# A hybrid decoder layer: value transposes six products earlier, and the down stage's first operands queued behind the last channel tile

## The chip, the cores and the metric

The kernel runs on one core of a Trainium2 chip. The metric is the device time of one execution in microseconds (us); less is better. The core's engines work side by side and wait for one another through semaphores: TensorE (PE in the profile, with its weight loads as PEld), VectorE (DVE), ScalarE (ACT), GpSimd (POOL) and SyncE (SP), which here issues all DMAs.

## What is computed

One decoder layer on 1040 tokens (16 learned meta tokens and 1024 of input), width 1024, all in float32. Two groups of four heads run side by side on one input projection: differential attention (two softmax maps, subtracted) and HGRN2 (a gated linear recurrence). Their outputs are joined, projected and added to the residual; a feed-forward layer with a short convolution follows. Cut to what matters:

```
a = rmsnorm(h, ln_mix_pre)
dq, dk, dv, hq, hf, hi, hg = jnp.split(a @ w_in, SPLITS, axis=-1)
mix = concat([diff_attention(dq, dk, dv, ...), hgrn2(hq, hf, hi, hg, ...)]) @ w_out
h = h + rmsnorm(mix, ln_mix_post)
u = rmsnorm(h, ln_ffn_pre) @ w_up                  # 1024 -> 2 x 2816
u = causal_conv_width_3(u) + conv_b                # per channel
gate, up = jnp.split(u, 2, axis=-1)
y = (gelu(gate) * up) @ w_down                     # 2816 -> 1024
return (h + rmsnorm(y, ln_ffn_post))[meta tokens dropped]
```

## The kernel before

Every float32 operand of a large product is split into a high part (a cast on ACT) and the rest (a subtraction on DVE or POOL), and each product is three matmuls: high by high, high by rest, rest by high. PE's order is the order in which the code issues its instructions (`manual_schedule`). The order of the other engines, SP's included, is planned when the program is built: among the instructions that are ready by the planner's own times, the one issued first in the code goes first, unless an edge holds it. `issue_after(x)` draws such an edge: what the block issues on the engine of `x` is queued behind `x`, without a wait for its end. `high_priority` moves a block ahead of what is issued before it. On the chip each engine then keeps its planned order. A tile gets a buffer of its tag in the same planning; its first writer waits until the tile that had the buffer is read out.

*The heads.* For each head a dense part (`dense`, L726) and a side part (attention or HGRN2) are interleaved on PE: each step of the side part is followed by dense products of about so much cost. The dense part computes transposed projections, tile by tile of 128 channels; a tile has three groups of tokens (`proj_group`, L191), a group 24 products (eight slices of the width by three matmuls, L203, L205 and L207) into a PSUM bank `pi_...`. For the value tiles, `dv` of the attention and `hi` of HGRN2, the result is copied to SBUF by ACT (`vt`, `ht`) and noted in a list `late`; `flush` (L369) later transposes it in blocks of 128 tokens on PE (`to_nat`, L311, products L317 and L319) into a bank `pn_va` or `pn_vh`, from which ACT copies it to its place (`avn`, `vn`). The flush of a group stands behind the 15th product of the group that comes next (`step == 14`, L734). The bank of the transposes is of the tag "m", which in this stage has two; the same tag serves the attention's late scores `E` (L639), its transposed probabilities `pt` (L666), its output `pa` (L690), the transposes of the normed outputs `ss` and `ssa` (L518), and HGRN2's `pk`, `pu` and `pl`. There are 24 flushes: two of head 0's `dv` stand in another function (`head0`, L900), four in the first group of a dense part, 18 elsewhere in `dense`.

*The up projection* works on 22 tiles of 128 channels of each half (`ft`, loop L1384), in two halves of the tokens `p`. From tile 1 on a tile is seven block products by a Strassen-like scheme (`unit`, L1305, steps j = 0 to 6, in `mm` L1311 twelve matmuls each) in the banks `pa`, `pb`, `pc`, which DVE and ACT combine between the steps (`u2` L1326, `u3` L1332, the copy of `ug` L1336). `prep` (L1077) casts and sums the weights of the next tile. At the end of a tile `gated` (L1279) convolves on ACT and DVE, multiplies on POOL and stores the result to DRAM (`gsc`, L1284). Beside tiles 6 to 20 `down_sums` (L1371) prepares sums of the down weights with buffers of the tag "gk".

*The down stage* has seven products by the same scheme (`ORDER`, L1400), each over 11 channel tiles: 77 steps, of 12 matmuls (L1483 to L1485). A step's operands (`operands`, L1433) are a tile of `gsc` (`g_in`, tag "gk", four buffers), a tile of weights (`w_in`, tag "ra", five buffers, which the up projection's raw weights use before), their casts `gh` and `wh` on ACT and the rests `gl` and `wl` on DVE; `gh` and `gl` have four buffers, `wh` shares four with the up projection. The code issues the operands of a step three steps ahead of its products (`ahead`, `LOOK`, L1548), those of the first three after the up projection's loop, the first with high priority. Between them `sums5` (L1427) loads three more tiles per channel tile. No edge holds these loads and casts, so that they go as early as the planner has buffers for them.

## Time and profile before

| | |
|---|---|
| median of 3 runs | 1334.59 us (1334.57 to 1335.59) |
| the profiled execution | 1334.41 us |
| its span, first to last instruction | 1332.6 us |
| its mean granted TensorE clock | 0.995 |
| head stage, with the joined output projection begun | about 60 to 560 us of the span |
| up projection | about 660 to 1106 us |
| down stage | 1106 us to the end |

Times in the views are counted from the start of the span. A group or row names line, engine, operation, the tile written and the tiles read; DVE, ACT and POOL instructions are recorded under the line of the helper that issues them (L54), so they are told apart by their tiles. A timeline row has start and duration in us, and in brackets the engine's idle time ahead of it with what ended it. Matmuls overlap in the pipeline, so their durations are longer than their distance.

### The profile page before, as it was taken

To read this page: it belongs to the slowest core of one execution; us is meant where nothing else is said; L and a number is where in the kernel's file an instruction comes from. 1 tells how busy PE (TensorE), PEld (TensorE's weight loads), DVE (VectorE), ACT (ScalarE), POOL (GpSimd) and SP (SyncE) were. 2 spreads that over 40 slices of the span, in tenths; PEclk is the share of its full clock that TensorE was granted. 3 is DMA by queue.
4 is the path that set the end of the run, shared out by engine and by line. 5 is a ranking of instruction groups with operands and counts; after the bars stand their busy time and mean duration, and the time that the engine had idled before them with its cause. 6 is when DMAs were issued, how large, how long until landed. Compare 5 with 4: busy or idle time off the path is not lost.

```text
span 1332.6 us, 26191 instructions
## 1 busy us (share of the span) xinstructions
PE 1288.0 (97%) x10172; PEld 1187.6 (89%) x10172; DVE 931.6 (70%) x1531; ACT 692.5 (52%) x1635; POOL 456.2 (34%) x340
## 2 busy tenths in 40 slices
PE   8999999999999999899999999999999989999997
PEld 7899999899999988677999999999999988878875
DVE  6464646465645664547997788988989886697586
ACT  8465466447544755246754444444444444454553
POOL 5211211121112110344076667677676630010121
PEclk9999999999999999999999999999999999999999
DMA  6111111112111234587232224545445436955363
GB/s 208 61 41 32 54 56 41 48 45 64 44 41 33 88 100 152 170 265 265 83 111 80 80 96 152 181 147 163 162 147 170 156 120 214 329 176 166 88 205 119
DMA packets 99427, 165.00 MB, mean 124 GB/s; under 512 B 10035, under 2 KB 34899, under 8 KB 99302
## 3 DMA queue, kind: packets, MB, share of 16 engines
q1 hardware_dynamic: 99302, 163.32, 37.8%
q8 instruction: 80, 1.31, 0.4%
q14 instruction: 45, 0.37, 0.1%
HBM read 122.65 MB, written 40.63 MB: 123 GB/s over the span
## 4 chain that ended last, share of the span: by engine, by line
PE 43%; DVE 10%; DMA 4%; issue 3%; ACT 3%; POOL 1%; SPq 0%; DVEq 0%; ACTq 0%; POOLq 0%
PE pd L1484 5%; PE pd L1483 5%; PE pd L1485 5%; PE pb L1316 4%; DVE c L54 3%; PE pb L1317 3%; PE pb L1318 3%; PE pa L1316 2%; PE pa L1317 2%; PE pa L1318 2%; PE pc L1316 2%; PE pc L1317 2%; PE pc L1318 2%; DMA gi<-gsc 1%; DVE ul L54 1%
## 5 line engine op out<-in xcount | busy, mean ns | idle before, releaser
L1316 PE MATMUL pb<-t,uh 128*128 128x258 f32 x504 | 144.8, 287 | 11.9 <-DVE u L54 11.8
L1317 PE MATMUL pb<-t,uh 128*128 128x258 f32 x504 | 142.3, 282 | 0.0
L1318 PE MATMUL pb<-t,ul 128*128 128x258 f32 x504 | 142.3, 282 | 0.0
L1484 PE MATMUL pd<-wl,gh 128*128 128x512 f32 x308 | 122.0, 396 | 0.5 <-DVE wl L54 0.5
L1483 PE MATMUL pd<-wh,gh 128*128 128x512 f32 x308 | 121.7, 395 | 0.0
L1485 PE MATMUL pd<-wh,gl 128*128 128x512 f32 x308 | 121.7, 395 | 0.0
L54 POOL TENSOR_TENSOR c<-c,c 128x514 f32<-128x514 f32 (+1 forms) x44 | 74.9, 1702 | 120.6 <-ACT c L54 110.3
L1316 PEld LDWEIGHTS pb<-t,uh 128*128 128x128 f32 x504 | 96.1, 191 | 15.2 <-DVE u L54 15.0
L54 DVE SCALAR_TENSOR_TENSOR c<-uu,cwt,c 128x514 f32<-128x514 f32 (+1 forms) x88 | 87.6, 1004 | 22.6 <-ACT c L54 22.3
L1317 PEld LDWEIGHTS pb<-t,uh 128*128 128x128 f32 x504 | 96.3, 191 | 0.0
L1318 PEld LDWEIGHTS pb<-t,ul 128*128 128x128 f32 x504 | 95.9, 190 | 0.0
L1316 PE MATMUL pa<-t,uh 128*128 128x258 f32 (+1 forms) x336 | 95.2, 283 | 0.0
L1318 PE MATMUL pa<-t,ul 128*128 128x258 f32 (+1 forms) x336 | 95.0, 283 | 0.0
L1317 PE MATMUL pa<-t,uh 128*128 128x258 f32 (+1 forms) x336 | 94.8, 282 | 0.0
L1316 PE MATMUL pc<-t,uh 128*128 128x258 f32 (+1 forms) x336 | 94.4, 281 | 0.0
L1317 PE MATMUL pc<-t,uh 128*128 128x258 f32 (+1 forms) x336 | 94.0, 280 | 0.0
L1318 PE MATMUL pc<-t,ul 128*128 128x258 f32 (+1 forms) x336 | 93.7, 279 | 0.0
L54 DVE SCALAR_TENSOR_TENSOR c<-ug,cwt,c 128x514 f32<-128x514 f32 (+1 forms) x88 | 88.2, 1002 | 1.5 <-ACT c L54 1.4
L54 ACT CAST uh<-ra 128x512 fp32r<-128x512 f32 x67 | 41.0, 616 | 67.9 <-PE pb L1317 49.7
L54 POOL TENSOR_TENSOR ul<-ws,uh 128x512 fp32r<-128x512 f32 x42 | 63.8, 1519 | 27.1 <-ACT uh L54 27.1
L1484 PEld LDWEIGHTS pd<-wl,gh 128*128 128x128 f32 x308 | 57.7, 187 | 15.8 <-DVE wl L54 1.9
L1483 PEld LDWEIGHTS pd<-wh,gh 128*128 128x128 f32 x308 | 57.7, 187 | 14.1
(373 smaller groups left out, 4169.5 us busy)
## 6 DMA issues: line engine op xcount, KB each, us to landing
ra<-in_wup_dram SPq DMA_DIRECT2D x88, 256.0 KB, 3.0
mp<-msc SPq DMA_DIRECT2D x23, 512.0 KB, 5.5
wd<-in_wdown_dram SPq DMA_DIRECT2D x44, 256.0 KB, 3.3
tsc<-wd SPq DMA_DIRECT2D x44, 256.0 KB, 3.1
wi<-tsc SPq DMA_DIRECT2D x44, 256.0 KB, 2.8
gi<-gsc SPq DMA_DIRECT2D x33, 256.0 KB, 3.6
wi<-in_wdown_dram SPq DMA_DIRECT2D x33, 256.0 KB, 4.2
gsc<-c SPq DMA_DIRECT2D x22, 257.0 KB, 2.3
```

The costliest lines, as they stand in the source:

```text
L54: ins = call(*args, **kw)
L1316: T.matmul(pt, hi[:, s], th[:, k], start=(first and k == 0), stop=False, skip_group_check=True)
L1317: T.matmul(pt, hi[:, s], tl[:, k], start=False, stop=False, skip_group_check=True)
L1318: T.matmul(pt, lo[:, s], th[:, k], start=False, stop=(k == 3), skip_group_check=True)
L1483: T.matmul(py, gh[:, s], wh, start=(k == 0 and pr not in (3, 7)), stop=False, skip_group_check=True)
L1484: T.matmul(py, gh[:, s], wl, start=False, stop=False, skip_group_check=True)
L1485: T.matmul(py, gl[:, s], wh, start=False, stop=(k == NH - 1), skip_group_check=True)
```

## The change

Two things. In `dense`, the flush stands behind the 9th product of a group, but for the first group of a dense part, where it stays behind the 15th.

For the down stage, the loads of the first three steps are issued at j = 1 of the last channel tile, on SP behind the store of the tile before it; their casts at j = 4, 5 and 6 of the last tile, on ACT behind the copy of `ug` of that tile's second half. The subtractions on DVE have no edge. The high priority of the first step goes. `ahead` no longer runs for the first three steps. The functions of the down stage are moved ahead of the loop for that, unchanged but for an argument of `operands` by which it takes loaded tiles.

```
             for g in range(3):
                 for step, c in enumerate(proj_group(g, parts, name, evac)):
-                    if step == 14:
+                    if step == (8 if idx or g else 14):
                         flush()
                     yield c
...
-        SY.dma_start(gsc[P * ft: P * (ft + 1), C0[p]:C0[p] + 2 * WN[p] - 2], cg)
+        marks["store"] = SY.dma_start(gsc[P * ft: P * (ft + 1), C0[p]:C0[p] + 2 * WN[p] - 2], cg)
...
-        A.copy(ug[:, :n], pa)
+        marks["left"] = A.copy(ug[:, :n], pa)
...
+    def operands(pr, k, loaded=None):
...
         if pr == 1:
-            a = g_in(k, 0, "1")
+            a = loaded[0] if loaded else g_in(k, 0, "1")
...
-        b = w_in(pr, k)
+        b = loaded[1] if loaded else w_in(pr, k)
...
             if (ft, j) == (1, 1):
                 with tc.issue_after(marks[1, 1].ins):
                     next(p1)
+            if ft == NF - 1 and j == 1:
+                with tc.issue_after(marks["store"].ins):
+                    opens = [(g_in(k, 0, "1"), w_in(1, k)) for k in range(LOOK)]
+            if ft == NF - 1 and j > 3:
+                with tc.issue_after(marks["left"].ins):
+                    ready[j - 4] = operands(1, j - 4, opens[j - 4])
...
     def ahead(i):
         if i < len(steps):
-            with tc.high_priority() if i == 0 else nullcontext():
-                ready[i] = operands(*steps[i])
+            ready[i] = operands(*steps[i])
...
-    LOOK = 3
-    for i in range(LOOK):
-        ahead(i)
     for i, (pr, k) in enumerate(steps):
         ahead(i + LOOK)
```

More of the change, by code (lines that the diff above doesn't have):

```diff
@@ L1381, in down_sums @@
                 yield
-    wd_sums = down_sums()
-    for ft in range(1, NF):
-        units = [unit(ft, p, ps_b) for p in range(2)]
-        for j in range(7):
-            prep(7 * (ft + 1) + j)
-            for u in units:
-                next(u)
-            if ft >= SUMS and j in (1, 3, 5, 6):
-                with tc.issue_after(marks["last"].ins):
-                    next(wd_sums, None)
-            if (ft, j) == (1, 1):
-                with tc.issue_after(marks[1, 1].ins):
-                    next(p1)
-    close(t2_cm, t_cm, xu_cm, mx_cm)
-    f_cm, fp = pool("fin", 1)
-    NH, TAIL = NF // 2, 3
-    ORDER = (1, 2, 5, 6, 3, 7, 4)
-    keep = {nm: fp.tile([P, NH, 512], F32, tag=nm, name=nm) for nm in ("ga", "gb", "gc", "gs")}
-    c11 = fp.tile([P, 4, 512], F32, tag="c11", name="c11")
-    x5 = fp.tile([P, 4, 512], F32, tag="x5", name="x5")
-    gfo = fp.tile([P, D], F32, tag="gfo", name="gfo")
-    ssd = fp.tile([P, 8, 2], F32, tag="ssd", name="ssd")
-    x1 = ep.tile([P, 4, 512], F32, tag="e0", name="x1")
-    u2 = ep.tile([P, 4, 512], F32, tag="e1", name="u2")
-    SY.dma_start(gfo, gfpost.to_broadcast([P, D]))
+    NH = NF // 2
+    LOOK = 3
+    ORDER = (1, 2, 5, 6, 3, 7, 4)
+    keep, ready = {}, {}
     def g_src(k, half):
@@ L1425, in w_in @@
         return t
-    def sums5(k):
-        SY.dma_start(keep["gc"][:, k], g_src(k, 1))
-        b = g_in(k + NH, 1, "5")
-        V.tensor_tensor(keep["gs"][:, k], keep["gc"][:, k], b, op=ALU.add)
-        SY.dma_start(keep["ga"][:, k], g_src(k, 0))
-    def operands(pr, k):
-        ga, gb, gc, gs = (keep[nm][:, k] for nm in ("ga", "gb", "gc", "gs"))
+    def operands(pr, k, loaded=None):
+        ga, gb, gc, gs = (keep[nm][:, k] if keep else None for nm in ("ga", "gb", "gc", "gs"))
         if pr == 1:
-            a = g_in(k, 0, "1")
+            a = loaded[0] if loaded else g_in(k, 0, "1")
         elif pr == 2:
@@ L1461, in operands, with sums5 @@
         return gh, gl, wh, wl
+    wd_sums = down_sums()
+    for ft in range(1, NF):
+        units = [unit(ft, p, ps_b) for p in range(2)]
+        for j in range(7):
+            prep(7 * (ft + 1) + j)
+            for u in units:
+                next(u)
+            if ft >= SUMS and j in (1, 3, 5, 6):
+                with tc.issue_after(marks["last"].ins):
+                    next(wd_sums, None)
+            if (ft, j) == (1, 1):
+                with tc.issue_after(marks[1, 1].ins):
+                    next(p1)
+            if ft == NF - 1 and j == 1:
[4 more added lines that the diff above has]
+                    ready[j - 4] = operands(1, j - 4, opens[j - 4])
+    close(t2_cm, t_cm, xu_cm, mx_cm)
+    f_cm, fp = pool("fin", 1)
+    TAIL = 3
+    keep.update({nm: fp.tile([P, NH, 512], F32, tag=nm, name=nm) for nm in ("ga", "gb", "gc", "gs")})
+    c11 = fp.tile([P, 4, 512], F32, tag="c11", name="c11")
+    x5 = fp.tile([P, 4, 512], F32, tag="x5", name="x5")
+    gfo = fp.tile([P, D], F32, tag="gfo", name="gfo")
+    ssd = fp.tile([P, 8, 2], F32, tag="ssd", name="ssd")
+    x1 = ep.tile([P, 4, 512], F32, tag="e0", name="x1")
+    u2 = ep.tile([P, 4, 512], F32, tag="e1", name="u2")
+    SY.dma_start(gfo, gfpost.to_broadcast([P, D]))
+    def sums5(k):
+        SY.dma_start(keep["gc"][:, k], g_src(k, 1))
+        b = g_in(k + NH, 1, "5")
+        V.tensor_tensor(keep["gs"][:, k], keep["gc"][:, k], b, op=ALU.add)
+        SY.dma_start(keep["ga"][:, k], g_src(k, 0))
     steps = [(pr, k) for pr in ORDER for k in range(NH)]
@@ L1466, in layer_kernel @@
         early.setdefault(min(3 + 3 * k, 2 * NH - 3 + k), []).append(k)
-    ready = {}
     def ahead(i):
         if i < len(steps):
-            with tc.high_priority() if i == 0 else nullcontext():
-                ready[i] = operands(*steps[i])
+            ready[i] = operands(*steps[i])
         for k in early.get(i, []):
```

## The prediction

> **What bounds the kernel now.** I read the page's head first, then the busy time by stage, then TensorE's (PE's) timeline for its idle places.

> ```profile
> span 1332.6 us, 26191 instructions
> PE 1288.0 (97%) x10172; PEld 1187.6 (89%) x10172; DVE 931.6 (70%) x1531; ACT 692.5 (52%) x1635; POOL 456.2 (34%) x340
> ```
> ```profile
> 60.00:440.00 380.00, 370.99 (x3713) 356.78 (x3712) 214.34 (x475) 210.76 (x615) 66.80 (x69) 1.00 0.16 47
> 1120.00:1150.00 30.00, 30.00 (x131) 24.07 (x130) 19.23 (x30) 15.28 (x27) 0.00 (x0) 1.00 1.02 366
> ```

> A row of the second view gives the stage, its length, then the busy time of PE, PEld, DVE, ACT and POOL, the granted clock, the DMA share and GB/s. PE is the bound: in the whole span it stands still for 44.6 us (1332.6 - 1288.0), for 9.0 (380.00 - 370.99) in most of the heads, for nothing in the first down steps although the DMA is full there. So the change can win only places where PE waits. Those that it touches:

> ```profile
> 105.21 0.55 PE L670 MATMUL pt<-ident,pb 128*128 128x128 f32 x3 [0.31 <-ACT vn L54]
> 116.16 0.66 PE L670 MATMUL pt<-ident,pb 128*128 128x128 f32 x4 [0.49 <-ACT pb L54]
> 174.15 0.33 PE L317 MATMUL pn_va<-ident,vt 128*128 128x128 f32 x1 [0.62 <-ACT kn L54]
> 238.65 0.55 PE L319 MATMUL pn_vh<-ident,ht 128*128 128x128 f32 x3 [1.67 <-ACT pb L54]
> 428.30 0.33 PE L317 MATMUL pn_va<-ident,vt 128*128 128x128 f32 x1 [0.62 <-ACT kn L54]
> 494.19 0.90 PE L319 MATMUL pn_vh<-ident,ht 128*128 128x128 f32 x3 [2.53 <-ACT pb L54]
> 1072.97 0.39 PE L1316 MATMUL pb<-t,uh 128*128 128x258 f32 x1 [3.47 <-DVE u L54]
> ```

> The bracket is PE's idle time before the row and who ended it. The value transposes (`pn`) wait not for their source (`ht`, `vt`) but for a PSUM bank: the tag "m" has two, and the transposes got the one from which ACT still had to read scores (`pb` is the exponent) or `kn`. The wait of 0.62 is there three times (first and last shown, heads 1 to 3), the one at 238.65 in head 2 as well.

> ```profile
> 493.70:497.20 3.50, 3.01 (x12) 3.02 (x13) 0.32 (x2) 1.44 (x6) 0.00 (x0) 0.51 0.33 81
> 1074.00:1077.40 3.40, 3.40 (x17) 3.28 (x16) 3.40 (x4) 0.00 (x0) 3.31 (x3) 0.50 0.59 188
> ```

> The two longest waits are each paid twice: around both the granted clock is half for some 3.4 us.

> **First edit: transposes after the 9th product instead of the 15th.** It moves 18 of the 24 flushes (12 of `hi`, 6 of `dv`) up by six products; nothing is added. Each is three transposes. What counts is which banks are busy at the new place.

> *Free places.* In the second `dv` group the 9th product lies four microseconds ahead of the 15th, in front of the products that fill both banks; the banks have been read out there, so the 0.62 goes: 3 x 0.62 = 1.9 us. At 105.21 another tile waits for the copy of the transposed block; that copy comes earlier, 0.3 us. The third `hi` flush of each head (in the first `hg` group), the first one of heads 1 to 3 and the second `dv` ones wait nowhere now, and a bank is free at their new place too: 0.

> *Heads 1 to 3, second `hi` flush.* Head 1:

> ```profile
> 234.03 0.34 PE L207 MATMUL pi_hi<-ahi,wl_hi 128*128 128x384 f32 x1
> 234.05 0.58 ACT L54 ACTIVATE ona<-ssa,sub 128x384 f32<-128x384 f32 x1 [1.03 <-PE ssa L537]
> 234.90 0.38 PE L694 MATMUL pa<-avn,az 128*128 128x128 f32 x2
> 235.08 0.62 ACT L54 CAST wh_dq<-wr_dq 128x512 fp32r<-128x512 f32 x1
> 235.87 1.23 DVE L54 TENSOR_TENSOR ast<-ast 128x1 f32<-128x1 f32 x1
> 238.40 0.20 ACT L54 ACTIVATION_READ_ACCUMULATOR pb<-E,ast 128x1 f32 x1
> 239.24 0.48 ACT L54 COPY vn<-pn_vh 128x384 f32<-128x384 f32 x1
> 240.22 0.39 PE L613 MATMUL E<-k,q 128*128 128x512 f32 x1
> ```

> The 9th product is at 234.03. Of the banks, one holds the scores E until 238.60 (read accumulator 238.40 + 0.20), the other `ssa` until 234.63 (234.05 + 0.58). The transposes should take the latter: start 234.7, a new wait of 0.5. Then four products (0.17 each), and `pa` wants a bank: the transposes' own, after its copy (0.48) that follows the cast ending 235.70: 236.2 instead of 234.90. From `pa` to the next E (240.22) now go 5.3 us, 1.67 of them the wait and 0.33 the transposes that no longer stand there: 3.3. So E comes at 239.5, 0.7 earlier, and with it the chain behind it. Twice (head 2 has the same rows): 1.4 us. Were the copy ahead of the cast, 1.2 each.

> ```profile
> 488.73 0.58 ACT L54 ACTIVATE ona<-ssa,sub 128x384 f32<-128x384 f32 x1 [0.26 <-PE ssa L537]
> 489.77 0.61 ACT L54 CAST woh<-wor 128x512 fp32r<-128x512 f32 x1
> 493.93 0.20 ACT L54 ACTIVATION_READ_ACCUMULATOR pb<-E,ast 128x1 f32 x1
> 497.05 0.45 PE L613 MATMUL E<-k,q 128*128 128x512 f32 x1
> ```

> Head 3 alike: transposes 489.4, copy done 490.9, `pa` 490.9, E at 490.9 + 3.3 = 494.2, just as its bank comes free (493.93 + 0.20). Now it is at 497.05: 2.85 us, of which the half clock is 1.3 (transposes to E: 2.86 here, 240.22 - 238.65 = 1.57 in head 1).

> *Head 0, second `hi` flush, goes the other way.*

> ```profile
> 111.56 0.20 ACT L54 ACTIVATION_READ_ACCUMULATOR pb<-E,ast 128x1 f32 x1
> 112.44 0.39 PE L613 MATMUL E<-k,q 128*128 128x512 f32 x1
> ```

> Here the 9th product stands behind `pa` and both banks are held, the scores' until 111.76. Transposes 111.8, then 0.33 + four products 0.7 + four score products 0.5: E at 113.3 instead of 112.44. The tile at 116.16 already waits for E's exponent, so it is 0.9 later: -0.9 us (between 0 and -1).

> Sum: 1.9 + 0.3 + 1.4 + 2.85 - 0.9 = 5.5 us.

> **Second edit: the down stage's first three loads and casts are queued late.** Nothing is added: 6 DMAs, 6 casts, 6 subtractions. Now they are hoisted into the 20th tile of the up projection:

> ```profile
> 1053.01 0.32 SPq L1415 DMA_DIRECT2D gi<-gsc  x1
> 1060.00 0.37 SPq L1424 DMA_DIRECT2D wi<-in_wdown_dram  x1
> 1074.59 3.70 SPq L1415 DMA_DIRECT2D gi<-gsc  x3
> 1099.20 7.95 SPq L1424 DMA_DIRECT2D wi<-in_wdown_dram  x2
> ```
> ```profile
> 1056.38 0.62 ACT L54 CAST gh<-gi 128x512 fp32r<-128x512 f32 x1 [3.45 <-DMA gi<-gsc]
> 1065.60 1.12 DVE L54 SCALAR_TENSOR_TENSOR c<-uu,cwt,c 128x510 f32<-128x510 f32 x1 [2.42 <-ACT c L54]
> ```

> ACT stands in a cast that waits for its load (3.45), the convolution behind such casts waits, DVE waits for ACT (2.42) and comes late to `u`, for which PE waits 3.47. Without the casts the tile should wait as the others do:

> ```profile
> L1316 PE MATMUL pb<-t,uh 128*128 128x258 f32 x216 | 62.9, 291 | 8.4 <-DVE u L54 8.3
> ```

> That is 18 tiles (12 such products each) between 660 and 1040 us: 8.4 / 18 = 0.47. So 3.0 us go, and the half clock: 17 products in 3.40 us, where 0.12 apiece would hold 28: 11 x 0.12 = 1.3. Together 4.3 us.

> What it costs: in front of the down stage,

> ```profile
> 1095.37 0.33 SPq L1284 DMA_DIRECT2D gsc<-c  x1
> 1100.63 0.37 ACT L54 COPY ug<-pa 128x256 f32<-128x256 f32 x1 [1.06 <-PE pa L1318]
> 1106.09 0.39 PE L1483 MATMUL pd<-wh,gh 128*128 128x512 f32 x1
> 1122.97 0.69 DVE L54 TENSOR_TENSOR gl<-gi,gh 128x512 fp32r<-128x512 f32 x1 [0.68 <-ACT gh L54]
> 1125.69 0.40 PE L1483 MATMUL pd<-wh,gh 128*128 128x512 f32 x1
> ```
> ```profile
> 1100.00:1106.00 6.00, 6.00 (x53) 6.00 (x52) 3.06 (x6) 3.06 (x5) 0.00 (x0) 1.00 0.14 46
> ```

> The loads stand behind the store of 1095.37 on SP, 10.7 us before the first down product, with the queue nearly empty; the casts behind the copy of 1100.63, 5.1 us (1106.09 - 1101.00) before it. DVE is free 2.94 of the 6 us before 1106, so the first two steps (four subtractions of 0.69) nearly fit, and the third has until 1111.7. What queues behind on ACT and DVE is the last tile's convolution, for which PE does not wait. The price is depth: by 1106 before has 8 `gi` and 9 `wi` loads out (first and last issue above). Later steps should not overtake them: buffers of a tag must go out in program order, since steps 3 to 6, with all four `gh`, would leave none for step 0 and PE would never come to free one. With 4 and 5 buffers, two of each refilled by 1106, after has 6 and 7. Four loads of 256 KB at 366 GB/s are 2.9 us of a DMA that is full from 1120 on. The thinnest cover is step 7: ready 1123.66, used 1125.69, 2.0 us. So -0.9 us (0 if DMA catches up sooner, -4.4 with 1.5 more for the third step). Edit two: 4.3 - 0.9 = 3.4 us.

> **Sum.** 5.5 + 3.4 = 8.9. The profiled execution took 1334.41 us (span 1332.6 and 1.8 around it), 0.2 under the median of 1334.59: **1325.5 us**.

> **Rivals.**

> *The bank comes from the wrong side (slower).* The order in which tiles take banks is fixed when the program is planned. DVE's minimum at 235.87 took 1.23 us; if the plan holds it for short, the exponent is planned ahead of the transposes' copy, and `pa` gets the scores' bank. Then `pa` waits until 238.65, E is at 242.0: 1.7 worse, twice; head 3 498.8, 1.75 worse. The idle time, 235.7 to 238.65, exceeds the 2.53 that cost the clock: 1.3 more, twice. Edit one: 2.2 - 0.9 - 3.4 - 1.75 - 2.6 = -6.5; with 3.4 from edit two 1337.5 us, or 1334.9 if the clock holds. It decides as soon as that copy is planned after the exponent. For it: ACT now does exponent, `pa`'s reads, copy, in that order. Against: the copy is ready at 235.2, before the minimum begins.

> *The down stage starves.* 4.4 instead of 0.9 us: 1329.0. For it the full DMA (1.02), against it that PE waits nowhere in those 30 us now (30.00 of 30.00).

> *The loads do not stay away.* If steps 3 to 6 take the freed buffers early, the casts stall ACT as now and edit two gives nothing: 1328.9. Against it the order of the buffers.

> *The half clock is not the waits' doing.* Then both windows stay, somewhere, though the waits go: 1.3 twice, 1328.1. Against it: in heads and up projection there are just these two, each at one of the two longest waits, and none at the 1.67. [...]

> **How the numbers follow.** Forecast 0.53; wrong bank 0.20, halved between 1334.9 and 1337.5; starving 0.13; loads not kept away 0.08; half clock that stays 0.04; anything else in the plan 0.02. The range 1320.5 to 1336.5 takes in the forecast with its terms at their better ends (1.0 more in heads 1 and 2, 0.9 in head 0, 0.9 at the opening, 0.47 in the 20th tile, and 1.7 for a further wait that goes) and most of the wrong bank. Measurement tells 0.2% (2.7 us) from no change. Faster 0.78 (forecast and the three milder rivals), same 0.11 and slower 0.11 (half of the wrong bank and of the rest each).

> **What would show it.** Right: no wait at the three `pn_va`; `pn_vh` of heads 1 to 3 waiting 0.5 for ACT's `ona`, `pa` for `vn` not `pb`; a longer wait before the fourth `pt` of head 0; a full granted clock throughout the heads and the up projection; first `gi` issue behind the second last pair of stores; no wait over 1 us at `pb`. Wrong: `pa` waiting for `pb`, a PE wait at L1483 to L1485 in the first ten down steps over 1 us, or a half clock in a new place.

## The result, and the profile after

| | before | changed |
|---|---|---|
| median | 1334.41 us (1332.09 to 1335.59, 6 runs) | 1323.12 us (1320.85 to 1325.68, 6 runs) |
| ratio | | 0.9915, 95% interval 0.9901 to 0.9929 |
| profiled execution | 1334.41 us, span 1332.6 | 1325.6 us, span 1323.8 |

The changed kernel is faster by 11.3 us in the medians. The two profiled executions differ by 8.8, for the changed kernel's was one of its two longest, 2.5 us above the median; where two executions of this program differ is shown with `e10`.

The head of the page of the changed kernel:

```profile
span 1323.8 us, 26191 instructions
PE 1286.8 (97%) x10172; PEld 1185.5 (90%) x10172; DVE 930.1 (70%) x1531; ACT 692.5 (52%) x1635; POOL 455.4 (34%) x340
```

As many instructions as before. PE stands still for 37.0 us instead of 44.6: 7.6 less. The other 1.2 of the 8.8 are busy time: within the work there is one half clock window now (clock 0.50 from 544.97 us), where there were two (from 493.74 and 1074.00).

The same kernel's busy time by stage (columns as in the prediction):

```profile
60.00:440.00 380.00, 375.47 (x3749) 361.53 (x3748) 214.64 (x485) 213.31 (x624) 67.48 (x69) 1.00 0.17 49
440.00:560.00 120.00, 113.25 (x1078) 99.01 (x1077) 67.39 (x140) 59.95 (x167) 20.72 (x18) 0.99 0.39 125
...
1120.00:1150.00 30.00, 30.00 (x131) 24.07 (x130) 19.17 (x30) 16.07 (x28) 0.00 (x0) 1.00 1.02 373
```

In most of the heads PE idles 4.5 us instead of 9.0. The clock is not full everywhere, though: 0.99 in the second row, as in that stretch before. In the first down steps PE still waits nowhere between 1120 and 1150 us. PE's rows at the places of the prediction, from its timeline:

```profile
111.38 0.55 PE L319 MATMUL pn_vh<-ident,ht 128*128 128x128 f32 x3 [0.58 <-ACT pb L54]
...
112.95 0.39 PE L613 MATMUL E<-k,q 128*128 128x512 f32 x1
...
233.88 0.55 PE L319 MATMUL pn_vh<-ident,ht 128*128 128x128 f32 x3 [0.32 <-ACT ona L54]
...
235.00 0.49 PE L694 MATMUL pa<-avn,az 128*128 128x128 f32 x2
...
475.79 0.49 PE L694 MATMUL pa<-avn,az 128*128 128x128 f32 x2 [0.58 <-DVE at L54]
...
483.30 0.50 PE L613 MATMUL E<-k,q 128*128 128x512 f32 x1 [0.67 <-DVE at L54]
...
544.70 1.72 PE L417 MATMUL pl<-hq,kr 128*64 128x64 f32 x16 [2.57 <-DVE hq L54]
...
1103.62 0.50 PE L1491 MATMUL pd<-wl,gh 128*128 128x512 f32 x1 [1.10 <-DVE wl L54]
```

The waits of 1.67, 1.65 and 2.53 are now 0.32 each, `pa` at 235.00 waits for nothing, and head 0 has the new wait (0.58). Four rows are not in the prediction: two in head 3 (475.79, 483.30), one in the last head's levels (544.70, with a half clock), one at the third down step (1103.62). The 20th tile of the up projection lies in this group, of all `pb` products by `uh` between 1040 and 1090 us:

```profile
L1316 PE MATMUL pb<-t,uh 128*128 128x256 f32 (+1 forms) x61 | 17.4, 285 | 0.2 <-DVE u L54 0.2
```

0.2 us of idle time in all (0.24 in one row), where one row had 3.47.

To put the time in its place I take the start of the same matmul before minus after, the *lead*. It rises where the change wins; times are those of the changed kernel but where the row says otherwise:

| place | forecast | change of lead |
|---|---|---|
| `pt` at 105.21 of before | 0.3 | 0.55 |
| head 0, second `hi` flush | -0.9 | -0.6 |
| first `dv` flush, heads 1 to 3 | 1.9 | three times 0.8: 2.5 |
| second `hi` flush, heads 1 and 2 | 1.4 | 1.2 + 1.2 = 2.4 |
| head 3 | 2.85 | 1.8 |
| levels of the last HGRN2 head (504 to 553) | 0 | 6.7 to 5.3: -1.4 |
| from there to the 20th tile of the up projection | 0 | -0.7 |
| 20th tile | 4.3 | 4.9 |
| first six down steps | -0.9 | -1.6 |
| a wait at 1179.76 of before that is gone | 0 | 0.75 |

From 1172 us on the lead stays at 8.7; the forecast's sum was 8.9.

### The profile page after: what moved, and what is told of

It reads as the page before. It is cut to its first block, busy times and chain, and to the rows that moved or that the text cites. A ratio compares the mean times of both kernels' runs of the same rounds, so it can differ in the third digit from the quotient of the medians.

```text
span 1323.8 us, 26191 instructions
## 1 busy us (share of the span) xinstructions
PE 1286.8 (97%) x10172; PEld 1185.5 (90%) x10172; DVE 930.1 (70%) x1531; ACT 692.5 (52%) x1635; POOL 455.4 (34%) x340
## 4 chain that ended last, share of the span: by engine, by line
PE 45%; DVE 11%; ACT 3%; issue 3%; DMA 2%; POOL 0%; SPq 0%; DVEq 0%; ACTq 0%; POOLq 0%
PE pd L1491 5%; PE pd L1492 5%; PE pd L1490 5%; DVE c L54 5%; PE pb L1316 4%; PE pb L1317 3%; PE pb L1318 3%; PE pa L1316 2%; PE pa L1317 2%; PE pa L1318 2%; PE pc L1316 2%; PE pc L1317 2%; PE pc L1318 2%; PE py L976 1%; PE py L972 1%
## 5 line engine op out<-in xcount | busy, mean ns | idle before, releaser
L1316 PE MATMUL pb<-t,uh 128*128 128x258 f32 x504 | 144.0, 286 | 8.9 <-DVE u L54 8.9
L1318 PE MATMUL pb<-t,ul 128*128 128x258 f32 x504 | 141.6, 281 | 0.0
L54 POOL TENSOR_TENSOR c<-c,c 128x514 f32<-128x514 f32 (+1 forms) x44 | 75.2, 1709 | 121.1 <-ACT c L54 111.4
L1316 PEld LDWEIGHTS pb<-t,uh 128*128 128x128 f32 x504 | 95.4, 189 | 12.2 <-DVE u L54 12.1
L54 DVE SCALAR_TENSOR_TENSOR c<-uu,cwt,c 128x514 f32<-128x514 f32 (+1 forms) x88 | 89.2, 1023 | 19.3 <-ACT c L54 19.0
L1318 PEld LDWEIGHTS pb<-t,ul 128*128 128x128 f32 x504 | 95.2, 189 | 0.0
L1316 PE MATMUL pa<-t,uh 128*128 128x258 f32 (+1 forms) x336 | 95.2, 283 | 0.0
L1318 PE MATMUL pa<-t,ul 128*128 128x258 f32 (+1 forms) x336 | 95.0, 283 | 0.0
L1316 PE MATMUL pc<-t,uh 128*128 128x258 f32 (+1 forms) x336 | 94.4, 281 | 0.0
L1318 PE MATMUL pc<-t,ul 128*128 128x258 f32 (+1 forms) x336 | 93.7, 279 | 0.0
L54 DVE SCALAR_TENSOR_TENSOR c<-ug,cwt,c 128x514 f32<-128x514 f32 (+1 forms) x88 | 89.6, 1019 | 0.9 <-ACT c L54 0.6
L54 ACT CAST uh<-ra 128x512 fp32r<-128x512 f32 x67 | 41.0, 616 | 66.4 <-PE pb L1317 48.2
L54 POOL TENSOR_TENSOR ul<-ws,uh 128x512 fp32r<-128x512 f32 x42 | 64.7, 1541 | 20.4 <-ACT uh L54 20.4
L1492 PEld LDWEIGHTS pd<-wh,gl 128*128 128x128 f32 x308 | 57.7, 187 | 14.4 <-DVE gl L54 0.4
```

The source lines that it names most:

```text
L54: ins = call(*args, **kw)
L1316: T.matmul(pt, hi[:, s], th[:, k], start=(first and k == 0), stop=False, skip_group_check=True)
L1318: T.matmul(pt, lo[:, s], th[:, k], start=False, stop=(k == 3), skip_group_check=True)
L1492: T.matmul(py, gl[:, s], wh, start=False, stop=(k == NH - 1), skip_group_check=True)
```

## The experiments

**Each edit by itself.** The kernel before with the first edit alone (`e1`):

```
-                    if step == 14:
+                    if step == (8 if idx or g else 14):
```

> The flush edit alone. Theory A (the gain is the sum of the places where PE no longer waits, and the two edits do not touch one another): the heads end 6 to 7 us earlier than before, as in the changed kernel; behind the last head 1.9 of that are lost in executions in which the wait of 2.6 us there brings the half clock; the wait of about 3.5 us at pb in the 20th up tile and its half clock stay. 4.5 to 7 us faster than before, ratio 0.995 to 0.9965. Theory B (the planner has reshuffled other engines as well, and part of the gain hangs on both edits being there): the heads gain less than 5 us, or the 20th tile's wait changes by over 1 us.

The changed kernel with the flush back at the 15th product (`e2`):

```
-                    if step == (8 if idx or g else 14):
+                    if step == 14:
```

> The down stage's opening alone, flush at the 15th product. Theory A: waits of the heads as before (1.67, 1.65, 2.53 and three of 0.62, half clock near 494 us), no wait over 1 us in the 20th up tile, a wait of about 1.1 us in the third down step; 3.5 to 4.5 us faster, ratio 0.9965 to 0.9975. The sum of this and the flush edit alone is the changed kernel's gain within 1.5 us. Theory B: under 2.5 us or over 6 us.

`e1` took 1326.87 us (ratio 0.9939, interval 0.9925 to 0.9954), `e2` 1329.9 (0.9964, 0.9952 to 0.9977). The gains, 7.5 and 4.5 us, add up to 12.0; both edits together gave 11.3. Each gain is known to about 2 us either way, and within that the parts add up, as Theory A has it. Two things fell outside it: `e1` won more than the 4.5 to 7 us expected, and the 20th tile's wait grew by 1.07, which by its wording is a sign of Theory B. PE's row there in `e1`:

```profile
1068.45 0.58 PE L1316 MATMUL pb<-t,uh 128*128 128x258 f32 x1 [4.54 <-DVE u L54]
```

4.54 instead of 3.47. Without the second edit that tile waits for casts that wait for their loads, and in this execution ScalarE stood 3.05 us in the second such cast, 1.82 before.

**What the transposes waited for.** The kernel before, flush at the 15th product, with another bank for the tag "m", at the cost of one for the input projections (`e5`):

```
-    deep.update(ip=2, m=2)
+    deep.update(ip=1, m=3)
```

> The kernel before, with three PSUM banks for the tag of scores, transposes and attention output, and one instead of two for the input projections. If a bank is what the value transposes wait for, the waits of 0.62 (heads 1 to 3, first dv flush), 1.67 (heads 1 and 2, second hi flush) and 2.53 (head 3) are gone or under 0.3 us, with the flush still at the 15th product. If they wait for their source, or only for ACT being late as such, they stay within 0.3 us of what they were. The total is not to be read: with one bank the projections wait for their own evacuation at every group, which should cost several per cent.

The groups of the transposes between 60 and 660 us, before:

```profile
L319 PE MATMUL pn_vh<-ident,ht 128*128 128x128 f32 x32 | 6.0, 291 | 5.8 <-ACT pb L54 5.8
...
L317 PE MATMUL pn_va<-ident,vt 128*128 128x128 f32 x3 | 1.0, 330 | 1.9 <-ACT kn L54 1.9
```

in `e5`:

```profile
L319 PE MATMUL pn_vh<-ident,ht 128*128 128x128 f32 x32 | 5.4, 272 | 0.0
...
L317 PE MATMUL pn_va<-ident,vt 128*128 128x128 f32 x3 | 0.8, 271 | 0.0
```

and in the changed kernel:

```profile
L319 PE MATMUL pn_vh<-ident,ht 128*128 128x128 f32 x32 | 5.7, 279 | 1.5 <-ACT ona L54 1.0 <-ACT pb L54 0.6
...
L317 PE MATMUL pn_va<-ident,vt 128*128 128x128 f32 x3 | 0.8, 271 | 0.0
```

The number behind the second bar is the idle time ahead of the group: 7.7 us before, 0.0 with a third bank, 1.5 after. With one more bank all of it goes while the transposes stay where they were in the group: it was the bank. `e5`, a single run, took 1486.58 us, since the projections now wait for their one bank (`pi_dq` alone 24.4 us); more time passes between scores and transposes there, so the run alone would be weak evidence. It agrees with the releasers: `pb` and `kn` read banks, not `ht` or `vt`. The source was there long before, too. In head 1 of the kernel before, ScalarE wrote `ht` in this row:

```profile
232.53 0.49 ACT L54 COPY ht<-pi_hi 128x384 f32<-128x384 f32 x1
```

It ends at 233.02, 5.6 us ahead of the transposes at 238.65.

**The place of the flush.** The changed kernel with the 12th product (`e7`) or the 6th (`e8`):

```
-                    if step == (8 if idx or g else 14):
+                    if step == (11 if idx or g else 14):
```

> The changed kernel, with the flush at the 12th product instead of the 9th. There the transposed block's copy on ScalarE stands behind the weight cast (0.62 us) in heads 1 and 2, as the prediction had it for the 9th product. If that order sets when pa gets its bank, pa waits some 1.2 us there, heads 1 and 2 give 0.7 each instead of 1.2, and the time is about 1 us over the changed kernel's: 1324. If at a later place pa instead takes the bank of the scores (the rival on record), pa waits 2.5 to 3 us for the exponent in heads 1 and 2, they lose 1.7 each, and the time is 1328 or more. If neither the order of copy and cast nor the place matters, 1323.

```
-                    if step == (8 if idx or g else 14):
+                    if step == (5 if idx or g else 14):
```

> The changed kernel, with the flush at the 6th product instead of the 9th. TensorE works in order, so where the transposes wait for the bank that ona leaves, going three products (0.5 us) earlier only makes that wait 0.5 longer (0.32 becomes 0.8 in heads 1 and 2) and E comes at the same time: within 1 us of the changed kernel, 1322 to 1324. If the place decides by the bank that is free there, an earlier place finds both banks busy: new waits over 1 us at pn_vh or pn_va and a time over 1326.

`e7` 1323.04 us (0.9918, 0.9896 to 0.9940), `e8` 1322.97 (0.9917, 0.9897 to 0.9936): neither can be told from the changed kernel by intervals 5 to 6 us wide. The waits differ. ScalarE in head 1 of the changed kernel, then of `e7`, then PE in `e7`:

```profile
234.47 0.48 ACT L54 COPY vn<-pn_vh 128x384 f32<-128x384 f32 x1
234.87 0.62 ACT L54 CAST wh_dq<-wr_dq 128x512 fp32r<-128x512 f32 x1
```
```profile
234.16 0.61 ACT L54 CAST wh_dq<-wr_dq 128x512 fp32r<-128x512 f32 x1
234.68 0.47 ACT L54 COPY vn<-pn_vh 128x384 f32<-128x384 f32 x1
```
```profile
235.20 0.49 PE L694 MATMUL pa<-avn,az 128*128 128x128 f32 x2 [0.72 <-ACT vn L54]
```

At the 12th product the weight cast stands ahead of the copy and `pa` waits 0.72 for it (1.2 was expected); at the 9th the copy goes first and `pa` waits for nothing. That is the branch of the prediction "were the copy ahead of the cast". In exchange the transposes of `e7` don't wait, so the two come out alike. In `e8` the second `hi` flush of heads 1 and 2 does not wait (0.8 was expected), but `ssa` behind it waits 0.40 for the bank, and the third flush 1.07 for `pb`, in the place of `pa`, which waits 0.82 there in the changed kernel; a wait over 1 us was named as the sign of the other theory, but it is that one moved, and the time over 1326 that should go with it did not come. At none of the three places does the `pa` behind the second `hi` flush of heads 1 to 3 wait for `pb`: the wrong bank of the prediction's rival did not happen there.

**What keeps loads and casts away from the 20th tile.** The changed kernel without the edge on the loads (`e3`), and without the one on the casts (`e4`):

```
-                with tc.issue_after(marks["store"].ins):
+                with nullcontext():
                     opens = [(g_in(k, 0, "1"), w_in(1, k)) for k in range(LOOK)]
```

> The changed kernel without the edge that holds the six opening loads behind the store; the casts stay behind the copy of ug. Theory A1 (the stall of the 20th up tile came from ACT standing in casts that waited for their loads, so the casts' edge does the work): no wait over 1 us in that tile though the loads go out 20 us and more earlier; time as the changed kernel within 2 us (1321 to 1326), the wait in the third down step stays. Theory A2 (the loads themselves disturb, by their place on SP or by the DMA): the wait of 3 us or more comes back, 1326 to 1329.

```
-                with tc.issue_after(marks["left"].ins):
+                with nullcontext():
                     ready[j - 4] = operands(1, j - 4, opens[j - 4])
```

> The changed kernel without the edge that holds the opening casts behind the copy of ug; the loads stay behind the store. Theory A1: the casts go as soon as the loads land (about 12 us before the down stage), in a tile in which ACT prepares no weights; no long wait anywhere, the third step's operands are ready earlier than in the changed kernel and its wait of 1.1 us shrinks or goes: 1320 to 1324. Theory A2 (the late loads already keep the casts away, so that the casts' edge only costs): 1 us faster than the changed kernel. A rival: casts that wait for loads stall ACT in the last tile, and PE waits over 1 us at pb there: 1325 to 1328.

`e3` 1322.85 us (0.9912, 0.9896 to 0.9927), `e4` 1322.81 (0.9914, 0.9899 to 0.9929): as fast as the changed kernel, and no wait over 0.25 us at the 20th tile in either. SP's first load for the down stage, in `e3` and in the changed kernel:

```profile
1046.63 0.32 SPq L1393 DMA_DIRECT2D gi<-gsc  x1
```
```profile
1063.55 21.39 SPq L1284 DMA_DIRECT2D gsc<-c  x4
1084.98 0.43 SPq L1393 DMA_DIRECT2D gi<-gsc  x1
```

In `e3` the load goes out 38 us earlier, as in the kernel before, and nothing is lost: either edge alone keeps the waiting casts out of the 20th tile. What hurt was a cast planned early *and* behind a load, not the load. In `e4` the opening loses its wait of 1.10, but PE waits in the last up tile, where VectorE's `u` stands behind a subtraction whose cast waits for its load (ScalarE 4.64 and 1.43 us at two of them), the old mechanism in small:

```profile
1089.02 0.39 PE L1316 MATMUL pb<-t,uh 128*128 128x258 f32 x1 [0.69 <-DVE u L54]
```

**The new wait in the levels.** The changed kernel with VectorE's subtractions for the second half of the output weights queued behind the last multiplication of the last level (`e6`):

```
-            V.tensor_tensor(qq[:, :, 1, :], ...)
+            halved[1:] = [V.tensor_tensor(qq[:, :, 1, :], ...)]
...
-                split(hi, lo, raw, V)
+                split(hi, lo, raw, V, halved[1] if n else None)
```

> The changed kernel, with VectorE's subtractions for the second half of the output weights (wol) queued behind the multiplications of the last level of the last head. If the wait of 2.57 us at 544.70 came from the subtraction that stands ahead of a level's multiplications and waits for a late load, it falls under 1.5 us, the half clock behind it goes, and the lead over before at the end of the heads is 7 to 9 us instead of 5.0: about 1320.5 us, ratio 0.990 or less. If the level waits for something else on that path (ScalarE's copies, the banks), a wait of 2 to 2.6 us stays there and the time stays at 1323. If the later subtractions hold the weight buffers and push the loads behind, new waits stand between 550 and 600 us and the time is over 1323.

Behind the wait of 2.57 in the changed kernel stand these rows, of VectorE, ScalarE and SP:

```profile
542.66 0.69 DVE L54 TENSOR_TENSOR wol<-wor,woh 128x512 fp32r<-128x512 f32 x1 [3.81 <-ACT woh L54]
543.27 0.69 DVE L54 TENSOR_TENSOR kr<-kr,tt 128x512 f32<-128x512 f32 x1
543.87 0.68 DVE L54 TENSOR_TENSOR hq<-hq,tt 128x512 f32<-128x512 f32 x1
```
```profile
542.01 0.62 ACT L54 CAST woh<-wor 128x512 fp32r<-128x512 f32 x1 [12.34 <-DMA wor<-in_wout_dram]
```
```profile
536.42 0.33 SPq L948 DMA_DIRECT2D wor<-in_wout_dram  x1
```

The level's `kr` and `hq` are behind a subtraction, that behind a cast, that behind a load: ScalarE stood 12.34 us for the load, VectorE 3.81 for the cast, PE 2.57 for `hq`. In `e6` VectorE does all levels first; VectorE, then ScalarE:

```profile
539.04 0.69 DVE L54 TENSOR_TENSOR kr<-kr,tt 128x512 f32<-128x512 f32 x1 [0.73 <-issue]
539.65 0.69 DVE L54 TENSOR_TENSOR hq<-hq,tt 128x512 f32<-128x512 f32 x1
...
542.75 0.69 DVE L54 TENSOR_TENSOR kr<-kr,tt 128x512 f32<-128x512 f32 x1 [1.66 <-issue]
543.36 0.68 DVE L54 TENSOR_TENSOR hq<-hq,tt 128x512 f32<-128x512 f32 x1
...
544.66 1.27 DVE L54 TENSOR_TENSOR wol<-wor,woh 128x512 fp32r<-128x512 f32 x2
```
```profile
540.14 0.62 ACT L54 CAST woh<-wor 128x512 fp32r<-128x512 f32 x1 [10.56 <-DMA wor<-in_wout_dram]
```

The level that stood at 543.27 in the changed kernel is the one at 539.04 here: it runs 1.1 us before that cast begins, and the subtraction comes behind the last level. The wait is gone, so is the half clock, and the lead at 553 us is 10.0 instead of 5.3. 1319.86 us (1319.66 to 1320.91, 4 runs; ratio 0.9892, 0.9877 to 0.9907).

**The wait at the third down step.** `e6` with that step's casts a product group earlier (`e9`), and beside it the changed kernel once more (`e10`, no edit):

```
-            if ft == NF - 1 and j > 3:
+            if ft == NF - 1 and j in (4, 5):
                 with tc.issue_after(marks["left"].ins):
-                    ready[j - 4] = operands(1, j - 4, opens[j - 4])
+                    for k in (0,) if j == 4 else (1, 2):
+                        ready[k] = operands(1, k, opens[k])
```

> The kernel with the subtractions behind the last level (the one of 1319.86 us), and with the third down step's casts queued at the sixth product of the last up tile, together with those of the second step, instead of at the seventh. If the wait of 1.10 us at the third down product comes from VectorE doing that step's two subtractions behind the convolution, it goes, no other wait over 0.5 us comes in the first ten down steps, and the time is 1318.8 us (1319.86 less 1.1), ratio about 0.988. If the loads are what is late (the price on record for the opening), the wait stays or moves to a step between the fifth and the eighth, and the time stays at 1319.9.

> The changed kernel as it is, profiled once more, beside the run above. In the ten profiles so far the half clock windows are 3.413 us long, start a whole number of 3.413 us apart within an execution, and follow a stretch of that length in which TensorE stood idle for 1.78 to 1.85 us or more in all. If it is such a stretch that counts, and its start has nothing to do with the program, the wait of about 2.5 us near 544 us costs the half clock in some executions (where 1.85 us of it lie in one stretch, about two in three) and not in others, and this profile has it or not for the same wait; the times scatter by some 1.3 us and more with it. If the wait's length alone decides, the window comes each time behind a wait of 2.5 us. Median 1323.1 us, ratio 0.9915.

VectorE ahead of the third step in the changed kernel, then PE in `e9`:

```profile
1100.56 1.80 DVE L54 SCALAR_TENSOR_TENSOR c<-ug,cwt,c 128x510 f32<-128x510 f32 x1
1102.28 0.68 DVE L54 TENSOR_TENSOR gl<-gi,gh 128x512 fp32r<-128x512 f32 x1
1102.88 0.68 DVE L54 TENSOR_TENSOR wl<-wi,wh 128x512 fp32r<-128x512 f32 x1
```
```profile
1100.93 0.50 PE L1492 MATMUL pd<-wl,gh 128*128 128x512 f32 x1 [0.57 <-DVE wl L54]
```

The last tile's convolution (`c`) stands ahead of both subtractions, and PE's product by `wl` starts at 1103.62. `e9` takes that wait away but the fourth step, now the first behind the convolution, waits 0.57. The expected case, no other wait over 0.5, did not come: in the trace half of the 1.10 was won, and the time, 1319.91 us (0.9889, 0.9869 to 0.9909), is the same as that of `e6`. `e10` took 1322.76 us (1321.84 to 1323.54, 6 runs) on the same chip, above all of `e9`'s five runs (1318.72 to 1320.46): the version with both mends beats the changed kernel by 2.9 us. Nearly all of that is `e6`'s edit.

The profiles of the changed kernel and of `e10` are of one program and 3.8 us apart in span (1323.8 and 1320.0). At 504 us the lead is 6.7 and 7.5, at 553 it is 5.3 and 7.9: by there 2.6 of the 3.8 are made, most of it in the levels. The wait expected near 544 is not in `e10`: the products that waited 2.57 at 544.70 start at 543.60 and wait for nothing. `e10` has one of 2.02 at 532.45 instead, with the half clock (0.50) behind it; what released that one the profile does not show.

## Why the prediction was right, step by step

It said 1325.5 us; the median is 1323.12, inside its range, and the profiled execution is 1325.6. The mechanism held where the edits touch PE's waits, and several sizes were off. That the sum came within 0.2 us of the lead is partly luck: its terms missed by up to 1.4 us, in both directions.

Not all signs that it named came. The wait before the fourth `pt` of head 0 is shorter, not longer (0.24, before 0.49; `pa` behind it waits another 0.24, for `pb`), `pa` of heads 1 and 2 waits for nothing instead of for `vn`, and the clock is not full throughout the heads. Of the signs of being wrong two came, a half clock in a new place and a wait over 1 us in the first ten down steps; the third, `pa` waiting for `pb`, came only with the 0.24 us in head 0 (the two waits of 0.82 were there before).

- *The bank, not the source*: shown, by the releasers, the time of `ht` and the third bank.
- *Free places*: 1.9 forecast, 2.5 of lead: the first transpose behind the wait had also taken 0.33 instead of 0.27 (the groups' mean ns above), and the rest, 0.15 each, I did not follow. The first `hi` flush of heads 1 to 3 was put at 0, and its transposes do wait nowhere. But in head 3 what follows them ahead of the second flush does: `pa` 0.58 and E 0.67, both for VectorE's copy of `at`. In front of the first such copy VectorE did this:

```profile
473.70 0.69 DVE L54 TENSOR_TENSOR wol<-wor,woh 128x512 fp32r<-128x512 f32 x1 [2.54 <-ACT woh L54]
474.31 0.97 DVE L54 TENSOR_REDUCE ast<-S 128x1 f32<-128x784 f32 x1
475.19 0.55 DVE L54 COPY at<-pt 128x384 f32<-128x384 f32 x1
```

  A subtraction of output weights again, waiting for its cast. The 0.58 is absent in `e7`, `e9` and `e10`. `e10` is the same program, so the wait is one of some executions; that it hangs on when the load lands is argued from these rows.
- *Heads 1 and 2*: 1.4 was worked out with the cast ahead of the copy. The chip had the copy ahead, and gave 2.4, the alternative that the text priced at 1.2 each.
- *Head 3*: 2.85 was too much by 1.0; these two waits, 1.25 together, lie in its stretch.
- *Head 0*: E at 112.95 where 113.3 was forecast, 112.44 before; -0.6 instead of -0.9.
- *The half clock goes with the waits*: it went at both places and came at a new one, which the text had named as a sign of being wrong. The 1.4 lost in the levels are that half clock: PE's idle time between 504 and 553 us is 4.1 us in all, and was 4.0 in the same stretch before (0.69 + 0.83 + 1.11 + 1.40), but no wait there had cost the clock. In `e10`, the same program, the stretch wins 0.4. The forecast looked only at waits that the edits touch; a lead also moves everything behind it against the loads.
- *The 20th tile*: 4.3 forecast, 4.9 found. The tile now waits 0.24 where 0.47 was forecast, 0.2 more, and the half clock had cost 1.7, not 1.3. The 17 products of the forecast are all those that touch the window; 15 start in it, some 0.21 us apart instead of 0.12.
- *The opening*: -0.9 forecast, -1.6 found, and not by the step that I named. 1.4 of it is the third step, which waits 1.10 for VectorE: the "1.5 more for the third step" that I had put only into the low end. Counting VectorE's free time (2.94 of 6 us) was too coarse: the subtractions had to fit in front of the convolution, not beside it. The depth of the loads, for which my 0.9 stood, was counted right (6 `gi` and 7 `wi` are out at the first down product), and step 7, the thinnest in the text, does not wait. But the sixth step loses 0.3, for its `gi` lands late; ScalarE in the changed kernel:

```profile
1111.13 1.29 ACT L54 CAST gh<-gi 128x512 fp32r<-128x512 f32 x2 [3.99 <-DMA gi<-gsc]
```

  In `e2` the sixth step loses 0.8; in `e3`, whose loads go early, nothing. That the lead ends only 0.9 below the 20th tile's is luck, for 0.75 come back at the 27th step, where the profile of before has this row:

```profile
1179.76 0.50 PE L1484 MATMUL pd<-wl,gh 128*128 128x512 f32 x1 [0.47 <-DVE wl L54]
```

  None of the other profiles has it, not even `e1`, which lacks the second edit. Whether it belongs to the program or to that one execution stays open.

## What to carry to other kernels

When a stream of work gains a lead, look at what stands on the other engines' queues in front of its next operands. In the levels here a cast waited 12.34 us for its load, the subtraction behind it 3.81, and PE 2.57 for what stood behind that. Free time in a window says nothing about that order: VectorE was free for 2.94 of the 6 us ahead of the down stage in the kernel before, and the third step of the changed kernel still waited 1.10 for it. The transpositions did not have to be placed to the product: at the 6th, 9th and 12th the kernel took 1322.97, 1323.12 and 1323.04 us, the same within what these runs tell apart (some 3 us). The 15th product, where the transposes took the bank that was read out last and waited 7.7 us in all, did not give that time (1329.9 in `e2`).

## What the runs showed of the hardware

In these profiles the half clock does not follow the length of a wait. The prediction's argument puts a bound between waits of 1.67 and 2.53 us; `e1` has a wait of 2.52 at 545.21 without it, `e8` a half clock behind one of 1.57 at 545.00. The half clock windows within the work last 3.413 us in the traces of the kernel before and the changed one (in `e1` the one from 1066.67 lasts two such lengths), and their starts in one execution lie a whole number of such lengths apart: the two of the kernel before (493.74 and 1074.00) 170.0, the changed kernel's (544.97) and the half clock behind its last products (1319.79) 227.0. The grids of two executions of one program, the changed kernel and `e10` (stretches from 541.56 and 529.21), are 3.62 lengths apart, so the program does not set the grid's start. So I added up PE's idle time in each stretch of that grid. Four stretches, each with the one that follows (the third number is PE's busy time, the third from the end the clock). The changed kernel, around its wait of 2.57:

```profile
541.56:544.97 3.41, 0.84 (x8) 0.33 (x7) 2.30 (x5) 2.60 (x6) 0.00 (x0) 1.00 0.82 301
544.97:548.38 3.41, 3.41 (x20) 2.25 (x19) 2.19 (x4) 0.13 (x1) 0.00 (x0) 0.50 0.45 163
```

`e1`, around its wait of 2.52:

```profile
541.00:544.40 3.40, 1.69 (x8) 0.41 (x5) 1.23 (x3) 1.86 (x5) 0.00 (x0) 1.00 0.83 261
544.40:547.80 3.40, 2.59 (x23) 1.98 (x24) 2.78 (x7) 1.16 (x3) 0.00 (x0) 1.00 0.75 279
```

and `e5`, the closest pair:

```profile
168.66:172.07 3.41, 1.56 (x71) 1.31 (x71) 1.11 (x2) 0.54 (x2) 0.00 (x0) 1.00 0.03 6
172.07:175.48 3.41, 3.41 (x17) 3.41 (x12) 1.76 (x4) 0.62 (x1) 1.20 (x5) 0.50 0.00 0
690.90:694.31 3.41, 1.58 (x12) 0.52 (x14) 0.74 (x2) 2.61 (x6) 0.00 (x0) 1.00 0.84 255
694.31:697.72 3.41, 3.41 (x47) 1.57 (x48) 2.04 (x4) 0.00 (x0) 0.00 (x0) 1.00 0.82 263
```

Behind 1.85 us idle (3.41 - 1.56) the clock of the next stretch was half, behind 1.83 it was full. The number of products does not part the two: 71 in the stretch behind which the clock fell, 12 in the other. In the kernel before the full clock was followed by half behind the stretches from 490.32, 1070.59 and 1323.17, with 2.08, 2.38 and 3.39 us idle, and by full behind all others, none with more than 1.65. Half followed 2.57 in the changed kernel and in `e7`, 2.76 in `e1`, 2.05 in `e8` and 2.02 in `e10`. One stretch does not fit: behind the last products of the changed kernel, 1.86 us idle, the clock stayed full in the next stretch.

```profile
1312.97:1316.38 3.41, 1.55 (x7) 0.93 (x5) 3.41 (x6) 2.19 (x7) 1.46 (x2) 1.00 0.50 198
```
